# Steps of the Hyena filters put behind every one and a half experts of the first expert stage

## The chip, the cores and the metric

The kernel runs on one core of a Trainium2 chip. The metric is the device time of one execution in microseconds (us); lower is better. A core has five engines that run side by side, each through its own list of instructions in order: TensorE (PE in the profile; its weight loads are shown as PEld), VectorE (DVE), ScalarE (ACT), GpSimd (POOL) and SyncE (SP). Semaphores order them against each other. Sixteen DMA engines move data between the main memory and the on-chip buffers; SyncE and GpSimd issue the transfers that matter here, each from a queue of its own.

## What is computed

Two transformer blocks on 256 tokens of width 1024, in float32. Every attention or mixing layer is followed by a mixture of experts. Two parts matter here.

The first expert stage, of the first block: a router picks 2 of 32 experts for each token, and each expert is a gated network with 512 hidden units.

```python
def expert_block(args):
    xb, e = args
    return (jax.nn.silu(xb @ w1[e]) * (xb @ w3[e])) @ w2[e]
```

The filters of the second block's Hyena layer: a small network of the position (33 features, three layers of 64 with sines) gives 2 x 2 filters for each of the 1024 channels; they are damped by a decay, normalised by their sum of absolute values, and convolved with the tokens much later. They depend on no token, so their spectra can be computed at any time before that layer.

## The kernel before

**Order of the stages.** Block 1 (attention and recurrence), the first expert stage (`moe_phase` with `l` None), the second block's attention, its expert stage (16 smaller experts), the Hyena layer, a third expert stage. The filters are computed inside the first expert stage, and the Hyena layer reads their spectra from a scratch tensor in main memory (`spectra`).

**The first expert stage.** The stage has 32 experts of 64 slots each (a rare overflow has a path of its own). The weights come through a ring of six buffers of 2 MB (`ring`, issued on SyncE at L1827 and L1853): per expert two buffers of up weights (w1 and w3) and, from the third expert on, one of down weights, half of those of an expert pair. A buffer is loaded again when TensorE has done its last matmul with it. For expert `e`, `up_unit` multiplies the gathered tokens by the up weights, 16 matmuls of 512 columns in four units (L288); `evac` copies the result on ScalarE (L293); `turn` transposes it on TensorE (L300); `silu` (L306, ScalarE) and `act` (L311, VectorE) form the hidden values; `down_unit` (L378) multiplies those of an expert pair by the down weights; ScalarE scales the rows (L367), and GpSimd sends them to main memory with an indirect transfer (L369). `gather` (L259) picks and normalises tokens with one-hot matmuls for eight experts at a time: for the first eight before the stage's experts begin, and for each later group among the matmuls of the last expert of the group before.

`Moe.run` writes this sequence out by hand. It is traced inside `manual_schedule()`, so its own order stays as written. Everything that is traced outside is placed by a planner, which follows data, buffers and its own estimates of time, and puts an instruction with nothing to wait for where the engine would otherwise be idle in its plan.

**The filters.** `moe_phase` is given a function `after`, here `filters`, and calls it once the sequence up to the last expert is traced. Its instructions are to come after two others of the same engine (`issue_after`): on TensorE after `m.ready`, the last matmul of the first gather, and on VectorE after `last`. `issue_after(i)` binds only those instructions that run on the engine of `i`. `filter_first` loads a Fourier matrix and the small network's weights, and computes the network (L1619). Then come 16 units, one for each of two filter orders and eight blocks of 128 channels. A unit (`filter_spectrum`) is a generator with three parts:

1. load w4 (64 KB, two buffers, L1630) and the decay `dec` (128 KB, one buffer, L1632), both from GpSimd's queue; two matmuls (L1635); multiply by the decay on VectorE (L1637); sums of absolute values on ScalarE (L1641); normalise, and form sum and difference on VectorE (L1642 to L1649);
2. four transposes (L1654) and a copy on ScalarE to `ftk` (L1656);
3. eight matmuls with the Fourier matrix (L1662), a copy on ScalarE (L1665) into a buffer of the tag `hd`, which has two buffers shared with part 1, and a write of 256 KB from GpSimd's queue to `spectra` (L1666).

`filters` runs 18 steps. Step `n` traces part 3 of unit `n - 2`, part 2 of unit `n - 1` and part 1 of unit `n`. The tiles of the filters lie in the pool `pl`. After it is closed, the pool `m1o` takes its space; it holds the gate row `g2row` and the buffers `vw` into which the experts' rows are read back at the end of the stage (L1951). A float32 matmul shows as two records in the trace, a transpose as one.

Of the kernel before, what the change touches and what calls it, by code (L numbers as in the profile page):

```python
# [29 lines left out]
CAP = 64  # L30
# [5 lines left out]
class Ctx:  # L36


    def __init__(self, tc, es):
        self.tc, self.nc = tc, tc.nc  # L40
        self.n = 0
        self.last = [None] * 3
        self.const = es.enter_context(self.pool("const"))
        self.ps = {}
# [42 lines left out]
def make_consts(k):  # L87
    nc, c = k.nc, k.const
    jp = k.t(c, [P, P], I32, "jp")
    nc.gpsimd.iota(jp, pattern=[[1, P]], base=0, channel_multiplier=-1)  # L90
    k.ident = k.t(c, [P, P], F32, "ident")
    nc.vector.tensor_scalar(k.ident, jp, 0.0, None, op0=ALU.is_equal)
    k.before = k.t(c, [P, P], BF16, "before")
    nc.vector.tensor_scalar(k.before, jp, 0.0, None, op0=ALU.is_gt)
    k.ones_bf = k.t(c, [P, P], BF16, "ones_bf")
    nc.vector.memset(k.ones_bf, 1.0)
    k.io64 = k.t(c, [P, CAP], F32, "io64")
    nc.gpsimd.iota(k.io64, pattern=[[1, CAP]], base=1, channel_multiplier=0, allow_small_or_imprecise_dtypes=True)
    k.io96 = k.t(c, [P, 96], F32, "io96")
    nc.gpsimd.iota(k.io96, pattern=[[1, 96]], base=0, channel_multiplier=0, allow_small_or_imprecise_dtypes=True)  # L100

    k.place = k.t(c, [P, 2, 2], F32, "place")
    nc.gpsimd.iota(k.place, pattern=[[T, 2], [P, 2]], base=1, channel_multiplier=1, allow_small_or_imprecise_dtypes=True)
    k.down = k.t(c, [P, 8], F32, "down")
    nc.vector.tensor_scalar(k.down, k.io96[:, :8], -1.0, 8.0, op0=ALU.mult, op1=ALU.add)
# [126 lines left out]
class Moe:  # L232


    def __init__(self, k, es, name, r, h2h, h2l, load, NE, FF, Y):
        self.k, self.nc, self.r = k, k.nc, r

        self.Y, self.ND = Y, NE // 2 - (1 if FF == 512 else 2)
        self.h2h, self.h2l = h2h, h2l
        self.load = load  # L240
        self.NE, self.FF, self.name = NE, FF, name
        self.sb = es.enter_context(k.pool(name + "sb", 2))
        self.acc = None
        self.first = True
        self.xg, self.oh, self.st = {}, {}, {}

# [27 lines left out]
    def x_of(self, e, c):  # L274
        g, i = divmod(e, GE)
        return self.xg[g][c][:, i * CAP:(i + 1) * CAP]

    def up_unit(self, e, u, w, x_of=None):


        s = self.state(e)
        if u == 0:
            s["p"] = self.k.bank()
        for j in range(2):
            c = 2 * u + j
            x = x_of(c) if x_of else self.x_of(e, c)
            for a in range(2):
                self.nc.tensor.matmul(s["p"][a * CAP:(a + 1) * CAP, :self.FF], x, w(a, c), start=(c == 0), stop=(c == 7))  # L288

    def evac(self, e):  # L290
        s = self.state(e)
# [544 lines left out]
def residual(k, pool, x, out, grow, h):  # L836

    nc = k.nc
    for t in range(2):
        tmp = k.t(pool, [P, 512], F32, "otmp", bufs=2)  # L840
        nc.vector.tensor_tensor(tmp, out[t], grow[:, h * 512:(h + 1) * 512], op=ALU.mult)
        xs = x[:, t, h * 512:(h + 1) * 512]
        nc.vector.tensor_tensor(xs, xs, tmp, op=ALU.add)
# [14 lines left out]
def row_in(k, pool, d, i, name):  # L858

    o = k.t(pool, [P, D], F32, name)  # L860
    k.nc.gpsimd.dma_start(o, d[i:i + 1].broadcast_to([P, D]))
    return o
# [891 lines left out]
def ffn_in(k, tmp, rp, x, M):  # L1754

    nc = k.nc
    r = rms_rows(k, rp, x, "rx")
    wr, NL = M["wr"], M["wr"].shape[2]
    pl = [k.bank() for _ in range(2)]
    xT = k.t(tmp, [P, 8, T], F32, "h2T")  # L1760
    for c in range(8):
        if c % 2 == 0:
            pb = k.acc()
        pt = pb[:, c % 2 * T:c % 2 * T + T]
        for t in range(2):
            nc.tensor.transpose(pt[:, t * P:(t + 1) * P], x[:, t, c * P:(c + 1) * P], k.ident)
        if str(c) in EVD:
            nc.vector.tensor_scalar(xT[:, c], pt, M["s"][:, c:c + 1], None, op0=ALU.mult)
        else:
            nc.scalar.activation(xT[:, c], pt, AF.Copy, scale=M["s"][:, c:c + 1])  # L1770
    for c in range(8):
        for t in range(2):
            nc.tensor.matmul(pl[t][:, :NL], xT[:, c, t * P:(t + 1) * P], wr[:, c], start=(c == 0), stop=(c == 7))  # L1773
    return pl, r
# [96 lines left out]
def moe_phase(k, I, x, l, M, after=None, store=None):  # L1871

    nc, tc = k.nc, k.tc
    NE, FF = (32, 512) if l is None else (16, 256)
    pre = "m1" if l is None else f"n{l}"
    with ExitStack() as es:
        ph = Phase(k, es)
# [35 lines left out]
        with ExitStack() as e1:  # L1913
# [9 lines left out]
            pl, r = ffn_in(k, tmp, rp if l is None else tmp, x, M)  # L1923
# [6 lines left out]
        with ExitStack() as e1:  # L1930
            m = Moe(k, e1, pre, R, h2h, h2l, load, NE, FF, Y)
            m.fetch = fetch
            m.scale, m.shift = M["s"], M["sh"]
            m.start(oh)
            with tc.issue_after(m.gathers.ins):
                R.gates()
            run = m.run()
            with (tc.manual_schedule() if str(l) in MAN else ExitStack()):
                next(run)
            if after:  # L1940
                with tc.issue_after(m.ready.ins), tc.issue_after(last.ins), ExitStack() as e2:
                    after(ph("pl", 2, es=e2))
            with (tc.manual_schedule() if str(l) in MAN else ExitStack()):
                list(run)
            op = m.vpool = ph(pre + "o", es=e1)
            with tc.issue_after(last.ins):
                g2 = row_in(k, op, M["g2"], 0, "g2row")
            for h, t in ((0, 0), (0, 1), (1, 0), (1, 1)):
                y, c = k.t(op, [P, 2, 512], F32, "vw", bufs=2), slice(h * 512, (h + 1) * 512)
                with tc.issue_after(m.sent.ins):  # L1950
                    nc.gpsimd.dma_start(y, Y.rearrange("(c t p) d -> t p c d", c=2, p=P)[t][:, :, c])  # L1951
                with tc.issue_after(m.acted.ins):
                    nc.vector.tensor_tensor(y[:, 0], y[:, 0], y[:, 1], op=ALU.add)
                    nc.vector.tensor_tensor(y[:, 0], y[:, 0], g2[:, c], op=ALU.mult)
                    nc.vector.tensor_tensor(x[:, t, c], x[:, t, c], y[:, 0], op=ALU.add)

            def add():
                for h in range(2):
                    residual(k, op, x, [m.acc[t][h] for t in range(2)], g2, h)
                    if store:  # L1960
                        store(h)

            add()
            m.overflow(add)
            k.newt = None
# [342 lines left out]
def body(tc, I, out):  # L2308
    nc = tc.nc
    with ExitStack() as es:  # L2310
        k = Ctx(tc, es)
        make_consts(k)
        k.ones = k.t(k.const, [P, P], F32, "ones")
        nc.vector.memset(k.ones, 1.0)
        x = k.t(es.enter_context(k.pool("xp")), [P, 2, D], F32, "xres")
        k.ada = [k.t(k.const, [P, 48], F32, f"ada{l}") for l in range(2)]
        k.scratch = tc.dram_tile([2, T, 8, 2, P], F32, name="spectra")
        b2 = Block2(k, I, x)
        M = {}

        def rows(m, name, pool, ada, j, *args):

            if j == 9:
                m.update(moe_prep(k, pool, name, *args))
            elif j == 11:
                m["g2"] = rows_out(k, pool, ada[:, 40:48], f"g2{name}")

        def prep1(b, j):
            rows(M.setdefault(None, {}), 0, b.pf, b.mod, j, k.col("norm2_w"), b.mod, k.wr[0], k.row("b1"))

        def prep2(m, l, pool, j):
            rows(m, 1 + l, pool, k.ada[l], j, b2.gffn[l], k.ada[l], k.wr[1 + l], k.row("b2")[:, 20 * l:20 * l + 20])

        block1(k, I, x, b2, prep1)
        def filters(pl):
            b2.filter_first(pl)
            units = [b2.filter_spectrum(pl, *divmod(n, 8), k.scratch) for n in range(16)]
            for n in range(18):
                for u in units[max(n - 2, 0):n + 1]:
                    next(u)  # L2340

        moe_phase(k, I, x, None, M[None], filters)
        M[0] = mla(k, I, x, b2, prep2)
        moe_phase(k, I, x, 0, M[0])
        M[1] = hyena(k, I, x, b2, prep2)

        def store(h):
            cols = slice(h * 512, (h + 1) * 512)
            nc.sync.dma_start(out.rearrange("b (t p) d -> p (b t) d", p=P)[:, :, cols], x[:, :, cols])

        moe_phase(k, I, x, 1, M[1], store=store)


# [16 lines left out]
```

## Time and profile before

| what | value |
|---|---|
| time, median of 3 runs | 1477.58 us |
| lowest and highest of them | 1474.06 and 1480.67 us |
| profiled execution, time | 1470.14 us |
| profiled execution, span from first to last instruction | 1468.4 us |
| mean granted TensorE clock, as a share of 2.4 GHz | 0.949 |
| TensorE busy | 1307.5 us (89% of the span) |
| VectorE busy | 532.4 us (36%) |
| ScalarE busy | 471.8 us (32%) |
| moved by DMA | 459.01 MB, mean 313 GB/s |

The profile is one execution on the chip, recorded by the hardware. "L288" is line 288 of the kernel. Busy time counts an engine's instructions and not its waits; matmuls overlap and their ends are modelled, so a TensorE that is busy all the time need not be at its peak. The time of the execution is 1.7 us longer than the span of its instructions. The first expert stage lies between about 300 and 850 us of the span.

### The profile page before, as it was taken

What the parts mean: (1) busy time and instruction counts of PE and PEld (TensorE: products, weight loads), DVE (VectorE), ACT (ScalarE), POOL (GpSimd) and SP (SyncE); (2) the same over time, 40 slices, a digit from 0 to 9 for tenths busy, and PEclk for the clock granted to TensorE, in tenths of its full rate; (3) what the DMA queues carried; (4) which work ended last, traced back from release to release, by engine and by line L of the source; (5) the groups of instructions that cost most, each with busy time, mean ns of one, the idle gap of its engine ahead of it and who ended that gap; (6) DMA issues with size and microseconds to landing.
All of it is one profiled execution on the core that took longest, in us unless ns stands there. A gap on an engine that the chain in (4) does not pass through costs nothing. (4 is left out here: it accounts for less than half of the span.)

```text
span 1468.4 us, 18609 instructions
## 1 busy us (share of the span) xinstructions
PE 1307.5 (89%) x7225; PEld 754.8 (51%) x7225; DVE 532.4 (36%) x1525; ACT 471.8 (32%) x903; POOL 90.0 (6%) x135
## 2 busy tenths in 40 slices
PE   5899999989989999988988568998997599988995
PEld 2676576653445553323322244656553588756552
DVE  2554655451322220000000267445002677673004
ACT  2473433341233322211211145434231444324321
POOL 0000000010111210000000100000001000000000
PEclk9899989999989999999999879998999699997998
DMA  8566724379999999999999867568999565729995
GB/s 318 197 206 243 295 92 171 131 275 429 411 367 347 357 336 412 426 423 427 424 425 425 317 244 270 174 229 355 421 422 413 211 259 196 277 91 418 421 417 231
DMA packets 64944, 459.01 MB, mean 313 GB/s; under 512 B 9638, under 2 KB 9942, under 8 KB 32720
## 3 DMA queue, kind: packets, MB, share of 16 engines
q1 hardware_dynamic: 52496, 424.97, 73.3%
q0 software_dynamic: 11920, 32.04, 5.7%
q8 instruction: 60, 0.98, 0.3%
q10 hardware_dynamic: 432, 0.72, 0.2%
q14 instruction: 36, 0.29, 0.1%
HBM read 440.89 MB, written 25.71 MB: 318 GB/s over the span
## 5 line engine op out<-in xcount | busy, mean ns | idle before, releaser
L288 PE MATMUL bank<-ring,xg 128*64 128x512 f32 (+1 forms) x2048 | 355.0, 492 | 20.1 <-DMA ring<-in_w_dram 15.6
L288 PEld LDWEIGHTS bank<-ring,xg 128*64 128x64 f32 x2048 | 142.8, 137 | 207.1 <-issue 137.6
L378 PE MATMUL bank<-ring,a 128*64 128x512 f32 x768 | 204.6, 601 | 7.4 <-DMA ring<-in_w_dram 7.4
L311 DVE TENSOR_TENSOR a<-bank,sg 128x256 f32<-128x256 f32 (+1 forms) x64 | 22.9, 358 | 476.1 <-ACT sg L306 292.4
L819 DVE TENSOR_TENSOR wl<-ra,wh 128x1024 fp32r<-128x1024 f32 (+1 forms) x77 | 93.3, 1216 | 74.5 <-ACT wh L817 73.8
L817 ACT ACTIVATE wh<-ra 128x1024 fp32r<-128x1024 f32 (+1 forms) x77 | 80.5, 1052 | 118.2 <-PE acc L832 39.9
L293 ACT ACTIVATE s<-bank 128x512 f32<-128x512 f32 (+1 forms) x64 | 31.4, 491 | 247.3 <-PE bank L288 247.3
L378 PEld LDWEIGHTS bank<-ring,a 128*64 128x64 f32 x768 | 55.3, 136 | 102.4 <-issue 88.2
L899 PE MATMUL fill<-rb,cpad 128*32 128x512 f32 x384 | 66.9, 653 | 22.7 <-DMA rb<-in_ada_w_dram 17.1
L269 ACT ACTIVATE xg<-bank,mcols 128x512 f32<-128x512 f32 x64 | 49.8, 778 | 66.6 <-PE bank L259 63.7
L367 ACT ACTIVATE y<-bank,gts 128x512 f32<-128x512 f32 x54 | 37.1, 687 | 75.1 <-PE bank L378 75.1
L1688 PE MATMUL acc<-hTh,wh 128*128 128x256 f32 x192 | 55.5, 292 | 0.0
L1688 PE MATMUL acc<-hTh,wl 128*128 128x256 f32 x192 | 55.3, 293 | 0.2 <-DVE wl L819 0.2
L1688 PE MATMUL acc<-hTl,wh 128*128 128x256 f32 x192 | 54.0, 284 | 0.0
L306 ACT ACTIVATE sg<-bank 128x256 f32<-128x256 f32 (+1 forms) x64 | 21.0, 328 | 90.3 <-PE bank L300 90.3
L259 PE MATMUL bank<-oh,h2h 128*128 128x512 f32 x128 | 46.1, 443 | 3.3 <-DVE oh L226 3.3
L300 PEld LDWEIGHTS bank<-ident,s 128*128 128x128 f32 x192 | 19.8, 140 | 46.3 <-issue 34.6
L1662 PE MATMUL acc<-ftk,dftf 128*128 128x128 f32 x256 | 36.0, 287 | 7.8 <-ACT ftk L1656 7.8
L259 PE MATMUL bank<-oh,h2l 128*128 128x512 f32 x128 | 42.5, 415 | 0.0
L832 PE MATMUL acc<-wh,hTh 128*128 128x512 f32 (+1 forms) x96 | 39.1, 408 | 3.6 <-ACT hTv L801 3.6
L1662 PEld LDWEIGHTS acc<-ftk,dftf 128*128 128x128 f32 x256 | 30.8, 192 | 22.2 <-ACT ftk L1656 12.1
L832 PE MATMUL acc<-wh,hTl 128*128 128x512 f32 (+1 forms) x96 | 38.5, 401 | 0.0
(679 smaller groups left out, 2061.4 us busy)
## 6 DMA issues: line engine op xcount, KB each, us to landing
ring<-in_w_dram SPq DMA_DIRECT2D x64, 2048.0 KB, 16.2
ring<-in_moe_w_in_dram SPq DMA_DIRECT2D x32, 2048.0 KB, 19.0
ring<-in_w_dram SPq DMA_DIRECT2D x62, 1024.0 KB, 18.4
rb<-in_ada_w_dram SPq DMA_DIRECT2D x48, 1024.0 KB, 6.8
ring<-in_moe_w_down_dram SPq DMA_DIRECT2D x32, 1024.0 KB, 19.3
rb<-in_w_mod_dram SPq DMA_DIRECT2D x16, 1024.0 KB, 7.3
ra<-in_hy_w_in_dram SPq DMA_DIRECT2D x12, 1024.0 KB, 7.8
ra<-in_w_in_dram SPq DMA_DIRECT2D x20, 512.0 KB, 3.6
```

The source lines that it names most:

```text
L259: i = nc.tensor.matmul(self.gp, h[:, t, c * P:(c + 1) * P], oh[:, t], start=(a == t == 0), stop=(a == t == 1))
L269: self.gathers = nc.scalar.activation(xg, self.gp, AF.Identity, scale=self.scale[:, c:c + 1], bias=self.shift[:, c:c + 1])
L288: self.nc.tensor.matmul(s["p"][a * CAP:(a + 1) * CAP, :self.FF], x, w(a, c), start=(c == 0), stop=(c == 7))
L293: self.nc.scalar.activation(s["s"], s["p"][:, :self.FF], AF.Copy)
L367: nc.scalar.activation(s["y"][:, h * 512:(h + 1) * 512], s["d", h], AF.Copy, scale=s["gt"])
L378: self.nc.tensor.matmul(q["d", h][i * CAP:(i + 1) * CAP], self.state(2 * p + i)["av"][:, c], w[:, i], start=(c == 0), stop=(c == nk - 1))
L817: k.last[0] = k.nc.scalar.activation(wh[:, :, :n], w, AF.Copy)
L819: k.last[1] = k.nc.vector.tensor_tensor(wl[:, :, :n], w, wh[:, :, :n].bitcast(F32), op=ALU.subtract)
L832: k.last[2] = k.nc.tensor.matmul(out, x, y[:, j, c0:c0 + n], start=(kt == 0 and a == 0), stop=(kt == KT - 1 and a == 2))
L899: nc.tensor.matmul(pr[32 * g:32 * g + 32], k.cpad[:, l, 4 * q + g], wq[:, g], start=(q == 0), stop=(q == 1))
L1662: nc.tensor.matmul(pt[:, (2 * f + n) * P:(2 * f + n + 1) * P], self.fwd[:, t, n, f * P:(f + 1) * P], tk[:, n, t], start=(t == 0), stop=(t ...
L1688: nc.tensor.matmul(acc[i][:, :T], y[:, jj, i * P:(i + 1) * P], self.hT[x][:, kt], start=(kt == 0 and a == 0), stop=(kt == 7 and a == 2))
```

## The change

`Moe` keeps, for each expert, the last up matmul that it traced (`mark`). `moe_phase` hands these to `filters`, and step `n` is traced with the order that it comes after the mark of expert 1 + 3n // 2: experts 1, 2, 4, 5, 7, 8 and so on, the last step behind expert 26. The mark is an instruction of TensorE, so the order holds for what a step does on TensorE. `filter_first` is traced as before, and the two orders that hold for all of `filters` stay.

```diff
@@ class Moe, __init__
-        self.acc = None
+        self.acc, self.mark = None, {}
@@ class Moe, up_unit
             for a in range(2):
-                self.nc.tensor.matmul(s["p"][a * CAP:(a + 1) * CAP, :self.FF], x, w(a, c), start=(c == 0), stop=(c == 7))
+                self.mark[e] = self.nc.tensor.matmul(s["p"][a * CAP:(a + 1) * CAP, :self.FF], x, w(a, c), start=(c == 0), stop=(c == 7))
@@ moe_phase
                 with tc.issue_after(m.ready.ins), tc.issue_after(last.ins), ExitStack() as e2:
-                    after(ph("pl", 2, es=e2))
+                    after(ph("pl", 2, es=e2), m.mark)
@@ body
-        def filters(pl):
+        def filters(pl, mark):
+
             b2.filter_first(pl)
             units = [b2.filter_spectrum(pl, *divmod(n, 8), k.scratch) for n in range(16)]
             for n in range(18):
-                for u in units[max(n - 2, 0):n + 1]:
-                    next(u)
+                with tc.issue_after(mark[1 + 3 * n // 2].ins):
+                    for u in units[max(n - 2, 0):n + 1]:
+                        next(u)
```

## Rows read from the trace of the kernel before

**Rows 1.** The profile's page, first line.

```profile
span 1468.4 us, 18609 instructions
```

**Rows 2.** Busy time by stretch: start:end, length, busy us (instructions), granted clock, DMA share, rate.

```profile
340.00:380.00 40.00, 40.00 (x182) 13.37 (x179) 9.58 (x25) 8.09 (x16) 1.69 (x3) 1.00 1.01 425
380.00:420.00 40.00, 32.97 (x157) 15.94 (x155) 9.30 (x29) 9.20 (x27) 8.03 (x12) 0.87 1.01 403
420.00:560.00 140.00, 139.23 (x707) 69.86 (x704) 32.68 (x99) 42.93 (x103) 25.51 (x38) 1.00 0.93 348
560.00:640.00 80.00, 79.38 (x366) 29.76 (x366) 3.77 (x13) 17.24 (x28) 3.00 (x3) 1.00 1.01 425
640.00:820.00 180.00, 156.68 (x667) 53.74 (x668) 6.99 (x21) 25.92 (x45) 5.83 (x6) 1.00 1.01 424
```

The five busy times are those of PE, PEld, DVE, ACT and POOL.

**Rows 3.** Waits of TensorE's matmuls, 420 to 560 us: total, times, longest.

```profile
PE acc L1662 <- ACT ftk L1656: 0.8, 1, 0.8
```

**Rows 4.** Waits of TensorE's matmuls, 640 to 820 us.

```profile
PE bank L288 <- DMA ring<-in_w_dram: 15.6, 18, 1.2
...
```

**Rows 5.** Matmuls of two lines of the filters, duration and first and last start.

```profile
L1635 PE MATMUL acc<-fh,w x64: 376/376/480, 378.5 to 536.4; 64*128 64x256 f32 x64
...
L1662 PE MATMUL acc<-ftk,dftf x256: 275/275/579, 385.7 to 550.9; 128*128 128x128 f32 x128
```

**Rows 6.** ScalarE in order of time, evacuations of experts 14, 17 to 19, 26, 27, 28, 31.

```profile
569.30 0.60 ACT L293 ACTIVATE s<-bank 128x512 f32<-128x512 f32 x1 [6.21 <-PE bank L288]
...
612.34 0.60 ACT L293 ACTIVATE s<-bank 128x512 f32<-128x512 f32 x1 [7.37 <-PE bank L288]
623.38 0.60 ACT L293 ACTIVATE s<-bank 128x512 f32<-128x512 f32 x1 [6.21 <-PE bank L288]
634.42 0.60 ACT L293 ACTIVATE s<-bank 128x512 f32<-128x512 f32 x1 [6.24 <-PE bank L288]
...
739.57 0.60 ACT L293 ACTIVATE s<-bank 128x512 f32<-128x512 f32 x1 [8.43 <-PE bank L288]
754.37 0.60 ACT L293 ACTIVATE s<-bank 128x512 f32<-128x512 f32 x1 [8.39 <-PE bank L288]
769.12 0.60 ACT L293 ACTIVATE s<-bank 128x512 f32<-128x512 f32 x1 [8.42 <-PE bank L288]
...
815.12 0.60 ACT L293 ACTIVATE s<-bank 128x512 f32<-128x512 f32 x1 [8.44 <-PE bank L288]
```

**Rows 7.** TensorE in order of time, one unit's worth and what follows it.

```profile
463.38 1.16 PE L1662 MATMUL acc<-ftk,dftf 128*128 128x128 f32 x8
...
467.05 3.65 PE L288 MATMUL bank<-ring,xg 128*64 128x512 f32 x16
```

**Rows 8.** DMA issues, 380 to 420 us: count, KB each, median us to landing.

```profile
ring<-in_w_dram SPq DMA_DIRECT2D x3, 2048.0 KB, 17.0
...
spectra<-hd POOLq DMA_DIRECT2D x3, 256.0 KB, 11.0
dec<-in_k_decay_dram POOLq DMA_DIRECT2D x4, 128.0 KB, 9.1
w<-in_hy_f_w_dram POOLq DMA_DIRECT2D x4, 64.0 KB, 7.8
```

**Rows 9.** DMA issues, 420 to 560 us.

```profile
ring<-in_w_dram SPq DMA_DIRECT2D x14, 2048.0 KB, 9.5
...
spectra<-hd POOLq DMA_DIRECT2D x13, 256.0 KB, 7.1
```

**Rows 10.** GpSimd's queue in order of time, the gate row.

```profile
552.81 0.57 POOL L861 DMA_DIRECT2D g2row<-g  x1
```

**Rows 11.** All engines in order of time, 406.5 to 408.5 us, a stall.

```profile
406.89 0.59 ACT L1665 COPY hd<-acc 128x512 f32<-128x512 f32 x1 [9.66 <-DMA spectra<-hd]
407.38 0.59 ACT L1656 COPY ftk<-acc 128x512 f32<-128x512 f32 x1
...
408.02 0.80 PE L1662 MATMUL acc<-ftk,dftf 128*128 128x128 f32 x2 [7.03 <-ACT ftk L1656]
```

**Rows 12.** Waits of all engines, 420 to 560 us.

```profile
DVE hd L1637 <- DMA dec<-in_k_decay_dram: 18.0, 4, 5.6
```

## Prediction

> **What bounds the kernel now.** The profiled execution takes 1470.14 us, of which 1468.4 us are span [rows 1]. I read the table of stretches first, over the first expert stage, because all edits lie there. The reader is to look at two columns, the DMA rate and TensorE's busy time [rows 2]. Three regimes show. From 340 to 420 us and from 560 to 820 us the core's DMA engines are full (share 1.01) and move 424 to 425 GB/s, with a dip to 403 between 380 and 420. From 420 to 560 they are not full: share 0.93, 348 GB/s, and there TensorE is busy for 139.23 of 140 us. From 640 on TensorE is busy for 156.68 of 180 us only, at a granted clock of 1.00, so it runs at 2.4 GHz and still has 23.3 us to spare.
>
> Then the waits of TensorE. Between 420 and 560 it waits for no weights; the one wait listed is 0.8 us for a filter's copy [rows 3]. Between 640 and 820 its longest wait in total is for the ring of expert weights [rows 4]. So the bound changes inside one stage: TensorE in the stretch with the filters, the weight stream elsewhere. The filters sit just there: first matmul of a unit at 378.5 us, last one at 550.9 us [rows 5].
>
> The pace of the experts gives the prices. ScalarE evacuates each expert once (L293). From 623.38 to 634.42 us is one expert with TensorE running through: 11.04 us. From 754.37 to 769.12 is one at the pace of the weights: 14.75 us. From 569.30 to 612.34 are three experts with a whole group's gather among them: 43.04 − 3 × 11.04 = 9.92 us for the gather, once in eight experts [rows 6].
>
> **The change, part by part.** Nothing is removed and no instruction is added: keeping the last up matmul of each expert in `mark` is bookkeeping at build time, and the argument `mark` costs nothing on the chip. What moves are 16 filter units in 18 steps. An order after expert 1 + 3n//2 is put on what step n issues on TensorE, the engine of the mark; its VectorE, ScalarE and GpSimd work, loads and writes included, follows by data and buffers alone.
>
> On TensorE, one unit's worth (16 of the 256 records of L1662, 4 of L1654, 4 of the 64 of L1635 [rows 5]) takes from 463.38 to 467.05 us, so 3.67 us, and 16 units 58.7 us [rows 7]. Per step in the steady state, with 1.5 experts: 1.5 × 11.04 + 3.67 + 9.92 × 1.5/8 = 22.1 us of TensorE. The weights of 1.5 experts take 1.5 × 14.75 = 22.1 us of DMA. A unit's own transfers are 256 + 128 + 64 KB [rows 8], 0.459 MB, which at 424.5 GB/s is 1.08 us, plus what they slow the stream by, below 0.6 us: 23.8 us. TensorE keeps 1.7 us of slack a step. So after the change the weight stream is the bound nearly throughout, and what TensorE does for the filters hides behind it. If that cover were gone, the 58.7 us would show.
>
> What can be won is what the DMA engines now lose: 40 × (1 − 403/424.5) = 2.0 us between 380 and 420, and 140 × (1 − 348/424.5) = 25.2 us between 420 and 560, together 27.2 us. The bytes stay the same, so the transfers' own time is in that already.
>
> What is won depends on why they lose it. Of the 25.2 us, (1.01 − 0.93)/1.01 × 140 = 11.1 us is idle engine time, because slots of the ring come free late; this goes away with TensorE's lag. The other 14.1 us are busy but slow. Two bounds. If all of it is the price of the filters' small transfers, it moves with them: between 420 and 560 there are 13 writes of spectra with their loads [rows 9], about 12 units by bytes, so 1.2 us a unit, 19.2 us for 16, and the gain is 27.2 − 19.2 = 8.0 us. If none of it is, the gain is 27.2 us. The nearest row to the state after the change is 380 to 420: filters beside a ring that is full of requests (a ring load lands 17.0 us after its issue there, 9.5 us between 420 and 560). There 3 writes, 4 decay loads and 4 weight loads were issued [rows 8], 1.57 MB or 3.4 units, and the loss is 2.0 us: 0.6 us a unit. I take that: 16 × 0.6 = 9.6 us, gain 27.2 − 9.6 = **17.6 us**.
>
> On this point the Trainium skill, "DMA: Bandwidth & Descriptors", Specifications, gives 512 bytes as the smallest transfer that still runs at line rate. The filters' pieces are runs of 512 bytes to 1 KB by the shapes in the code, so by that rule a unit costs its bytes alone and the gain would be 27.2 us. The 403 GB/s of the row say that this is too kind.
>
> Edits I cost at nothing, with their cover. The three tensors a unit loads are issued from GpSimd's queue, which also sends each expert pair's result rows (L369) and the gate row g2row. With a step every 22 us these stand between issues that are one step apart; dec has a single buffer, and its next load can go out once the VectorE product (L1637) is done, with 14.75 us at least before the next step and 9.1 us to landing [rows 8]. Queued behind that product on VectorE is the experts' L311, for which the down matmuls wait. g2row now goes out at 552.81 us, behind the filters [rows 10]; its buffer reuses their space, so it will go out behind the last step, after expert 26. That one is evacuated at 739.57 us now, and the last expert at 815.12 [rows 6], so g2row will still be there some 70 us before the stage's closing sums need it. The first steps cannot follow experts 1, 2 and 4: the features they need end at 378 us, beside expert 5, and I expect steps 0 to 3 close together there, as now. That costs nothing while the ring is full. The stall in that place, 7.03 us of TensorE behind a ScalarE copy that waits 9.66 us for an earlier spectrum's write [rows 11], stood in a stretch where the DMA share was 1.01, so losing it adds nothing to the 17.6 us.
>
> Against the profiled execution: 1470.14 − 17.6 = 1452.5 us. The median of the three runs shown, 1477.58 us, lies 7.4 us above that execution; the forecast for a median is 1477.6 − 17.6 = **1460 us**.
>
> **The rivals.**
>
> *The transfers carry their full price along* (no measurable change, 0.5% being 7.4 us, about what a measurement of this kernel can tell from nothing). 1.2 us a unit or somewhat more, gain 0 to 8 us, 1470 to 1478. For it: from 460 to 560 the DMA engines are nearly full and still slow. Against it: the same transfers cost half of that beside a full ring, and the wait that disappears is idle time as well. 0.18.
>
> *The transfers cost only their bytes*: gain 27 us, 1450. This is also what the 512 bytes of the Trainium skill's page would give. Against it stands the dip to 403. 0.10, counted with the faster ones.
>
> *Each step makes TensorE wait* (slower). Its queue is in order; a step's matmul that waits for ScalarE, VectorE or a load holds the experts behind it. Place: L1662 behind the copy L1656, and L311 behind L1637 waiting for dec. It has 1.7 us of slack a step. Beyond that every us costs 16 us: from 2.8 us a step the gain is gone, from 3.3 us the kernel is slower by over 0.5%. With the longest wait of VectorE for dec in the profile, 5.6 us [rows 12], at every step: 16 × (5.6 − 1.7) − 17.6 = +45 us, 1522. For it: such waits exist now. Against it: they come from units packed two to an expert, and the change puts at least one expert between two steps. 0.10.
>
> *The change does not spread them as it says.* The mark is only a lower bound, and a step goes where the written order of TensorE has room; steps that slide behind the last expert would show at 3.67 us each, so five of them would eat the gain: 1478, more of them slower. Against it: the steps now fill the places where TensorE later waits for the ring, and these places recur at every expert up to the last. 0.04.
>
> **How the numbers follow.** Forecast, with a loss of 0.3 to 1.2 us a unit, gain 8 to 22 us: 0.58. The rival in which steps slide is split by how many do: 0.02 still gain, 0.01 come out even, 0.01 slower. Faster by over 0.5%: 0.58 + 0.10 + 0.02 = 0.70. Within 0.5%: 0.18 + 0.01 = 0.19. Slower: 0.10 + 0.01 = 0.11. The predicted time is the forecast's, 1460 us. The range reaches from the full 27.2 us (1450) to almost no gain (1476); what it leaves out is slower cases and the last bit of the first rival.
>
> **What would show it.** Right: between 340 us and the end of the stage no long stretch under 410 GB/s; units' matmuls from about 380 to 720 us; experts evenly at 14.8 to 16.5 us; expert 31 evacuated near 797 us, not 815.12; every later stage earlier by the same amount. The price of the transfers shows as the DMA rate with filters against 424 after them. Wrong: waits at L1662, L1637 or L311 of several us per step, a clock below 1.00 in the stage, units after the last expert, or 400 GB/s and less with a full share for as long as the filters run.

## The result, and the profile after

The kernel with the change takes 1454.7 us (median of 4 runs, 1450.3 to 1460.1), the one before 1478.88 us (median of 4, 1474.06 to 1480.67). The ratio is 0.9851, with a 95% interval of 0.9820 to 0.9882: 22 us less, with 17 to 27 us in the interval. The forecast was 17.6 us less, 1460 us.

The two profiled executions differ by less, 1470.14 and 1460.1 us. That lies within the scatter from run to run: the one before was shorter than all of its four timed runs, the one after the longest of its four. The stage itself is a better measure, so I use one number from here on: the **stage time**, from the evacuation of the first expert to that of expert 31 on ScalarE (L293). Before it is 815.12 [rows 6] − 329.96 = 485.2 us. After, in ScalarE's order of time:

```profile
332.65 0.60 ACT L293 ACTIVATE s<-bank 128x512 f32<-128x512 f32 x1 [6.06 <-PE bank L288]
...
409.31 0.58 ACT L1665 COPY hd<-acc 128x512 f32<-128x512 f32 x1 [9.59 <-DMA spectra<-hd]
...
509.08 0.60 ACT L293 ACTIVATE s<-bank 128x512 f32<-128x512 f32 x1 [5.39 <-PE bank L288]
520.18 0.60 ACT L293 ACTIVATE s<-bank 128x512 f32<-128x512 f32 x1 [6.24 <-PE bank L288]
535.99 0.60 ACT L293 ACTIVATE s<-bank 128x512 f32<-128x512 f32 x1 [5.45 <-PE bank L288]
...
799.11 0.60 ACT L293 ACTIVATE s<-bank 128x512 f32<-128x512 f32 x1 [8.43 <-PE bank L288]
```

799.11 − 332.65 = 466.5 us, 18.7 us less. The stage began 2.7 us later in this execution, so its end stands 16.0 us earlier; the rest of the way to the span's end, through stages whose code is the same, gives 6 us back (653.3 us before, 659.2 after). In the twelve other executions below this rest takes 654.6 to 662.4 us, so the 6 us are scatter:

```profile
span 1458.3 us, 18601 instructions
```

The table of stretches, in the columns of [rows 2] and with the same first five stretches, then three that cut the last one finer:

```profile
340.00:380.00 40.00, 40.00 (x184) 13.33 (x182) 8.69 (x23) 8.26 (x16) 1.64 (x2) 1.00 1.01 424
380.00:420.00 40.00, 35.18 (x163) 15.56 (x160) 10.62 (x32) 9.88 (x28) 7.23 (x11) 0.91 1.01 405
420.00:560.00 140.00, 140.00 (x660) 60.74 (x656) 19.29 (x58) 36.50 (x75) 15.67 (x22) 1.00 1.01 414
560.00:640.00 80.00, 80.00 (x388) 33.71 (x388) 11.55 (x36) 18.08 (x40) 9.60 (x13) 1.00 1.01 415
640.00:820.00 180.00, 163.38 (x735) 62.31 (x733) 17.49 (x48) 32.72 (x63) 13.56 (x17) 1.00 0.97 404
...
640.00:700.00 60.00, 59.69 (x275) 25.02 (x274) 6.55 (x18) 16.20 (x33) 5.26 (x7) 1.00 1.01 421
700.00:740.00 40.00, 40.00 (x196) 16.37 (x196) 3.60 (x15) 6.53 (x15) 3.05 (x4) 1.00 1.01 425
740.00:800.00 60.00, 50.02 (x212) 16.18 (x211) 2.02 (x6) 7.54 (x14) 2.04 (x2) 1.00 1.01 424
```

The DMA share is 1.01 from 340 to 800 us: the hole of 0.93 and 348 GB/s between 420 and 560 us is gone. What is left is a shallow dip to 414, 415 and 421 GB/s while filters run, and 424 to 425 once they are done. The 404 in the fifth row is no dip: its last 20 us lie behind the end of the stage. What the dip costs, from these rows: 40 × (1 − 405/424.5) + 140 × (1 − 414/424.5) + 80 × (1 − 415/424.5) + 60 × (1 − 421/424.5) = 1.8 + 3.5 + 1.8 + 0.5 = 7.6 us. Of the 27.2 us that the DMA engines lost before, that leaves 19.6 us, and the stage shows 18.7.

The waits of TensorE's matmuls from 420 to 700 us, the whole list (before, [rows 3] and [rows 4]):

```profile
PE bank L288 <- DMA ring<-in_w_dram: 0.3, 1, 0.3
```

TensorE is busy without a gap, the DMA engines are full, and neither waits for the other. The two bounds have met. The units are spread as written, from 381.2 to 728.4 us, where [rows 5] ended at 550.9:

```profile
L1635 PE MATMUL acc<-fh,w x64: 375/376/481, 381.2 to 698.4; 64*128 64x256 f32 x64
...
L1662 PE MATMUL acc<-ftk,dftf x256: 274/275/378, 388.4 to 728.4; 128*128 128x128 f32 x128
```

Where the time came from is seen in the intervals between the evacuations of neighbouring experts (us, read from ScalarE's order of time):

| from expert | before | after |
|---|---|---|
| 0 to 5 | 8.4, 7.7, 11.0, 11.8, 14.5 | 8.4, 7.7, 11.0, 11.8, 14.5 |
| 5 to 13 | 31.2, 23.5, 17.9, 22.5, 20.8, 21.6, 21.3, 16.1 (174.9) | 27.2, 17.0, 18.7, 17.6, 11.1, 15.8, 15.8, 11.1 (134.2) |
| 13 to 31 | 11.0 to 18.4 (256.9) | 11.1 to 20.2 (278.9) |

Experts 5 to 13 give 40.7 us, experts 13 to 31 take 22.0 us back.

### The profile page after: what moved, and what is told of

Read it like the earlier page. It is cut to its first block, busy times and chain, and to the rows that moved or that the text cites. A ratio compares the mean times of both kernels' runs of the same rounds, so it can differ in the third digit from the quotient of the medians.

```text
span 1458.3 us, 18601 instructions
## 1 busy us (share of the span) xinstructions
PE 1310.4 (90%) x7225; PEld 757.7 (52%) x7225; DVE 532.4 (37%) x1525; ACT 471.0 (32%) x903; POOL 90.5 (6%) x135
## 5 line engine op out<-in xcount | busy, mean ns | idle before, releaser
L378 PE MATMUL bank<-ring,a 128*64 128x512 f32 x768 | 207.0, 607 | 2.9 <-DMA ring<-in_w_dram 2.9
L293 ACT ACTIVATE s<-bank 128x512 f32<-128x512 f32 (+1 forms) x64 | 31.3, 490 | 240.3 <-PE bank L288 240.3
L378 PEld LDWEIGHTS bank<-ring,a 128*64 128x64 f32 x768 | 55.5, 137 | 94.7 <-issue 85.6
L300 PE MATMUL bank<-ident,s 128*128 128x128 f32 x192 | 35.4, 294 | 6.7 <-ACT s L293 6.7
L832 PE MATMUL acc<-wl,hTh 128*128 128x512 f32 (+1 forms) x96 | 38.5, 401 | 0.0
## 6 DMA issues: line engine op xcount, KB each, us to landing
ring<-in_w_dram SPq DMA_DIRECT2D x64, 2048.0 KB, 20.2
```

Source lines behind the costliest of these rows:

```text
L293: self.nc.scalar.activation(s["s"], s["p"][:, :self.FF], AF.Copy)
L300: self.nc.tensor.transpose(pm[:, c * P:(c + 1) * P], s["s"][:, c * P:(c + 1) * P], k.ident)
L378: self.nc.tensor.matmul(q["d", h][i * CAP:(i + 1) * CAP], self.state(2 * p + i)["av"][:, c], w[:, i], start=(c == 0), stop=(c == nk - 1))
L832: k.last[2] = k.nc.tensor.matmul(out, x, y[:, j, c0:c0 + n], start=(kt == 0 and a == 0), stop=(kt == KT - 1 and a == 2))
```

## The experiments

Twelve kernels, each against the kernel before on the same chip. A stage time is from one profiled execution. Experts 20 to 31 took 165.7 to 166.6 us in the five kernels with no filter work left there (before, 5, 7, 8 and 10), so differences of about 1 us between stage times are read as none.

| kernel | median, us | ratio to before, 95% | stage, us |
|---|---|---|---|
| before | 1476.3 to 1478.9 | 1 | 485.2 |
| after | 1454.7 | 0.9851 [0.9820, 0.9882] | 466.5 |
| 1 one step per expert | 1467.03 | 0.9945 [0.9921, 0.9968] | 477.1 |
| 2 after, four experts later | 1457.57 | 0.9867 [0.9833, 0.9902] | 464.8 |
| 3 after, less TensorE work | 1456.75 | 0.9868 [0.9838, 0.9899] | 465.5 |
| 4 after, half the decay loads | 1456.32 | 0.9864 [0.9837, 0.9891] | 463.1 |
| 5 after, no filters | 1433.81 | 0.9702 [0.9665, 0.9739] | 440.7 |
| 6 after, no transfers of the units | 1439.62 | 0.9736 [0.9697, 0.9776] | 448.2 |
| 7 before, no transfers of the units | 1464.56 | 0.9907 [0.9876, 0.9939] | 474.8 |
| 8 before, less TensorE work | 1480.66 | 1.0018 [0.9996, 1.0040] | 490.1 |
| 9 one step per expert, from expert 5 | 1454.41 | 0.9837 [0.9814, 0.9859] | 465.4 |
| 10 before, three writes fewer | 1472.12 | 0.9960 [0.9942, 0.9978] | 479.3 |
| 11 experiments 2 and 4 together | 1453.71 | 0.9836 [0.9812, 0.9859] | 461.8 |
| 12 after, every spectrum written twice | 1469.74 | 0.9955 [0.9933, 0.9976] | 476.1 |

### 1. One step behind every expert

```diff
-                with tc.issue_after(mark[1 + 3 * n // 2].ins):
+                with tc.issue_after(mark[1 + n].ins):
```

> The steps come one behind every expert instead of one behind every one and a half, so the units are over by expert 16. Stage time below means from the first to the last expert's evacuation: 485.2 us before, 466.5 us after the change. Theory (TensorE's lag was the loss, and a unit costs the weight stream about 1.6 us wherever it stands): an expert then takes TensorE 11.04 + 3.67 + 1.24 = 16.0 us and the stream 14.75 + 1.6 = 16.4 us, so the stream is still the bound: stage 464 to 470 us, ratio to the kernel before 0.982 to 0.990. Rival (the density of small transfers slows the stream): the density lies half way between before and after, so about half of the gain is gone: stage 474 to 478 us, ratio 0.991 to 0.996.

More than half of the gain is gone, 10.6 of 18.7 us of the stage, about as the rival said. But the density is not shown to be the reason, because the kernel is not what I had in mind: the features are ready only beside expert 5, when the marks of experts 1 to 4 are past. Eight units land on experts 5 to 8, with intervals of 30.9, 23.5 and 17.9 us, those of before; behind them each expert has one unit and takes 15.8 us. The stretches behind the pile:

```profile
420.00:460.00 40.00, 40.00 (x194) 19.93 (x193) 6.17 (x17) 14.86 (x31) 5.99 (x9) 1.00 0.87 339
460.00:560.00 100.00, 100.00 (x489) 43.62 (x487) 20.47 (x63) 22.91 (x58) 15.37 (x23) 1.00 1.01 405
```

### 9. One step behind every expert, from the fifth

```diff
-                with tc.issue_after(mark[1 + 3 * n // 2].ins):
+                with tc.issue_after(mark[5 + n].ins):
```

> One step behind every expert again, but from expert 5 on, so that the first eight units no longer stand at experts 5 to 8. The run with one step per expert from expert 1 on had a stage of 477.1 us, and its experts 5 to 8 were as long as those of the kernel before. Theory (the loss there was TensorE's lag at the bunched units, 10 us; elsewhere one unit per expert costs TensorE 11.04 + 4.75 + 1.24 = 17.0 us against 16.4 us of the stream, and the ring covers that small lag): stage 465 to 471 us. Rival (one unit per expert is too dense for the DMA engines): 474 to 479 us, as with the first of these.

The same density without the pile, and the stage is as short as after's:

```profile
420.00:560.00 140.00, 140.00 (x670) 61.94 (x670) 23.92 (x72) 37.49 (x84) 19.47 (x28) 1.00 1.01 413
```

With experiment 1 this shows what the change cures: a pile of units on few experts puts TensorE behind the stream of weights, buffers of the ring come free late, and the DMA engines go short (0.87 there, 1.01 here). One and a half experts per step or one makes no difference here. Experiment 1 also has the stall of [rows 11] ahead of its pile, 6.7 us of TensorE, and this one has not; by experiment 10 that is worth some 4 of the 11.7 us between the two.

### 2. The same spread, four experts later

```diff
-                with tc.issue_after(mark[1 + 3 * n // 2].ins):
+                with tc.issue_after(mark[5 + 3 * n // 2].ins):
```

> All steps are moved four experts later, with the same spacing: they no longer bunch at experts 5 and 6, and the stall of several us behind a spectrum's write with the lower clock after it should vanish. Theory (the stall stands where the stream is the bound anyway, so it costs nothing): stage 464 to 469 us as after the change, ratio 0.982 to 0.989. Rival (the stall and the clock are part of the remaining loss): stage 457 to 461 us, ratio 0.976 to 0.981.

After still has the stall of [rows 11], 9.59 us of ScalarE at 409.31 in the rows above, and TensorE's granted clock is 0.91 in that stretch, with 35.18 of 40 us busy: behind the stall it is at the 1.2 GHz level for a while (eight records of L378 take 3.68 us, 1.89 us just ahead of it). Four experts later it does not occur: the interval 5 to 6 is 13.1 us and not 27.2. The stage gains 1.7 us, little more than a stage time can tell, so after the change the stall is hidden.

### 10. Before, with the first three writes left out

```diff
-        nc.gpsimd.dma_start(scratch[o][:, c].rearrange("(f p) n d -> p f (n d)", f=2), sp.rearrange("p f n d -> p f (n d)"))
+        if 8 * o + c > 2:
+            nc.gpsimd.dma_start(scratch[o][:, c].rearrange("(f p) n d -> p f (n d)", f=2), sp.rearrange("p f n d -> p f (n d)"))
```

> The kernel before without the writes of the first three spectra (left out; the Hyena layer reads other data of the same size). The ScalarE copy for which TensorE stood 7.03 us at expert 6 then has no write to wait for, and the clock should not fall there; 0.79 MB fewer are written. Theory (a stall ahead of the stretch in which TensorE is the bound makes TensorE late for all of that stretch): stage 7 to 10 us shorter, 475 to 478 us, all of it in the interval between the evacuations of experts 5 and 6. Rival, which the forecast held (the stall stands where the stream is full and is hidden): only the bytes, 2 us: stage 483 us.

Before the change the same stall was not free. Without the writes that cause it the interval 5 to 6 falls from 31.2 to 25.6 us and the next one by 0.7 us, the others up to expert 18 stay, and the stage is 5.9 us shorter. That lies between the two forecasts. The bytes left out, 0.79 MB, are 1.9 us of it at 424.5 GB/s. The rest is DMA time that is no longer lost where TensorE is the bound: 360 GB/s between 420 and 560 us in place of the 348 of [rows 2], which is 140 × 12/424.5 = 4.0 us.

```profile
420.00:560.00 140.00, 139.23 (x709) 69.53 (x709) 32.11 (x99) 42.55 (x102) 25.49 (x39) 1.00 0.95 360
```

The granted clock from 380 to 420 us is 1.00 here, 0.87 in [rows 2]. TensorE's longest wait from 380 to 470 us is now another one, so the gain is less than the 7.03 us of the stall:

```profile
PE acc L1654 <- DVE fs L1648: 2.9, 1, 2.9
```

### 7. Before, without the units' transfers

```diff
-        nc.gpsimd.dma_start(w4, self.I["hy_f_w4_2"][0]. ...)
-        nc.gpsimd.dma_start(dec, self.I["k_decay"][c * P:(c + 1) * P])
+        if o == c == 0:  (both loaded once, and kept for all units)
...
-        nc.gpsimd.dma_start(scratch[o][:, c]. ...)
...
-                        nc.sync.dma_start(K[o, h], k.scratch[o] ...)
+                        nc.sync.dma_start(K[o, h] ..., I["k_decay"] ...)
```

> The kernel before without the units' transfers, in the same way. On TensorE the units stand at experts 5 to 12 as in the kernel before. Theory (there TensorE's lag was the bound): TensorE is late all the same and the weights wait for their buffers; only what the units waited for their loads goes: stage 470 to 480 us, ratio 0.990 to 0.997. Rival (the small transfers, packed together, made the DMA engines slow, and moving them apart is what the change won): the loss goes with the transfers: stage under 460 us, ratio under 0.983.

All intervals are those of before but 5 to 6, 21.7 us in place of 31.2. So TensorE alone sets the pace of experts 6 to 13, whatever the transfers do. And the DMA engines are short *and* slow without them:

```profile
380.00:420.00 40.00, 40.00 (x206) 20.77 (x202) 11.73 (x36) 12.30 (x32) 1.01 (x1) 1.00 1.00 423
420.00:460.00 40.00, 40.00 (x194) 19.20 (x191) 7.80 (x23) 14.04 (x30) 0.99 (x1) 1.00 0.87 339
460.00:560.00 100.00, 99.22 (x513) 48.37 (x512) 22.56 (x69) 26.63 (x67) 3.50 (x4) 1.00 0.82 314
```

Divided by its share, a full set of engines would move 390 and 383 GB/s behind 420 us here, 374 in [rows 2] between 420 and 560 us, and 420 where the ring is full of requests. Some three quarters of the slowness per busy engine are there without the units' transfers beside the ring. From 380 to 420 us, where the ring is full of requests, it is the other way: 423 GB/s here against 403 before (405 in experiment 10, with most of the transfers and without the stall), so that dip, from which the forecast took its 0.6 us a unit, is the transfers'.

### 6. After, without the units' transfers

The edit is that of experiment 7, in the kernel after.

> The changed kernel without the units' transfers: the weights and the decay of one unit are loaded once and used by all, no spectrum is written, and the Hyena layer reads other data of the same size. All of TensorE's, VectorE's and ScalarE's work stays. Theory (the stream is the bound and a unit costs it 1.6 us): the stage falls nearly to the floor without filters, 437 to 445 us, though TensorE (22.1 us a step) and the weights (22.1 us) are then equal: ratio 0.967 to 0.973. Rival (TensorE is the bound after the change): stage stays within 5 us of 466 us, ratio 0.982 or more.

18.3 us less, between the two forecasts, and not the 25.8 us that leaving out the filters altogether gives (experiment 5; 24.6 of them are the filters' own), because TensorE takes over. From expert 7 to expert 27 every interval is that of after to within 0.5 us: in both kernels TensorE sets the pace there. The gain sits at the two ends, 7.4 us at experts 5 to 7, where the stall is gone with the writes, and 10.2 us behind expert 27, where TensorE after the change waits for the ring again (9.3 us from 730 to 800 us). No matmul waits from 420 to 700 us, and the DMA engines have some room:

```profile
460.00:560.00 100.00, 100.00 (x472) 41.91 (x470) 13.43 (x37) 25.16 (x52) 3.88 (x4) 1.00 0.99 412
640.00:770.00 130.00, 129.31 (x606) 51.41 (x604) 9.48 (x31) 27.30 (x53) 5.44 (x6) 1.00 1.00 413
```

### 3. After, with less work on TensorE

```diff
-        pt = k.fbank()
-        (the four transposes of L1654 and the copy to ftk)
...
-        (the eight matmuls of L1662 and the copy of L1665)
+        sp = hd.rearrange("p d (n c) -> p d n c", n=2)
```

> The changed kernel without the second and third part of each unit on TensorE and ScalarE (the transposes, the Fourier matmuls and their copies are left out; what is written as the spectrum is the filter itself, so the Hyena layer gets other numbers). All transfers stay. TensorE has 42 us less to do in the stage. Theory (TensorE's filter work is hidden behind the stream): stage 463 to 468 us, as after the change, ratio 0.981 to 0.988. Rival (TensorE still sets part of the time): stage down by 10 us or more, under 457 us, ratio under 0.978.

No gain beyond what a stage time can tell (1.0 us). The time freed on TensorE turns into waits for the ring, 420 to 700 us:

```profile
PE bank L288 <- DMA ring<-in_w_dram: 20.4, 16, 4.1
```

The DMA rate stays near after's 414 GB/s, so the dip there does not come from a TensorE that is late:

```profile
420.00:560.00 140.00, 129.39 (x540) 47.67 (x538) 19.43 (x59) 29.58 (x63) 16.75 (x23) 0.98 1.01 416
```

So in the kernel after the stream sets how long the stage takes, and TensorE's filter work is hidden, but, by experiment 6, only just.

### 5. After, without the filters

```diff
-        moe_phase(k, I, x, None, M[None], filters)
+        moe_phase(k, I, x, None, M[None])
...
-                        nc.sync.dma_start(K[o, h], k.scratch[o] ...)
+                        nc.sync.dma_start(K[o, h] ..., I["k_decay"] ...)
```

> The changed kernel without any filter work in the stage; the Hyena layer reads other data of the same size instead of the spectra. This is the floor of the stage. Theory (after the change the filters cost only their transfers, 16 x 1.6 us and 1 to 2 us for the first loads): stage 466.5 - 27 = 437 to 442 us, ratio about 0.967. Rival (TensorE's 58.7 us are partly paid too): stage under 430 us, ratio under 0.960.

```profile
420.00:560.00 140.00, 126.48 (x551) 44.78 (x548) 7.03 (x24) 21.91 (x36) 4.85 (x5) 1.00 1.01 426
```

The stream alone runs at 426 GB/s. After's filters cost 466.5 − 440.7 = 25.8 us; before the change they cost 44.5 us. Some of that is not theirs: without them the gate row's transfer of 512 KB, 1.2 us at 424.5 GB/s, goes out at 302.20 us, ahead of the stage. That leaves 24.6 us, 1.54 us a unit.

### 4. After, with each decay block loaded once

```diff
-        dec = k.t(pool, [P, T], F32, "dec", bufs=1)
-        nc.gpsimd.dma_start(dec, self.I["k_decay"][c * P:(c + 1) * P])
+        if o == 0:
+            self.dec = k.t(pool, [P, T], F32, "dec", bufs=1)
+            nc.gpsimd.dma_start(self.dec, self.I["k_decay"][c * P:(c + 1) * P])
+        dec = self.dec
...
-            units = [b2.filter_spectrum(pl, *divmod(n, 8), k.scratch) for n in range(16)]
+            units = [b2.filter_spectrum(pl, n % 2, n // 2, k.scratch) for n in range(16)]
```

> The changed kernel with the units in the order block by block, both filter orders of a block one after the other, so that the decay of a block is loaded once and used twice: 8 loads of 128 KB fewer, the same arithmetic. Theory (the stream is the bound, each byte of the filters is paid): 8 x 0.131 MB at 424.5 GB/s is 2.5 us, with their share of the slowing 3 to 4 us: stage 462 to 464 us, ratio 0.3% below that of the change, 0.980 to 0.986. Rival (the small loads are hidden, only the writes slow the stream): stage 466 us, no difference from the change.

Eight loads fewer, 1.05 MB or 2.5 us at 424.5 GB/s, and the stage is 3.4 us shorter (experiment 11 against 2: 3.0). The times of the whole kernel can't tell so little.

### 12. After, with every spectrum written twice

```diff
         nc.gpsimd.dma_start(scratch[o][:, c].rearrange("(f p) n d -> p f (n d)", f=2), sp.rearrange("p f n d -> p f (n d)"))
+        nc.gpsimd.dma_start(k.scratch2[o][:, c].rearrange("(f p) n d -> p f (n d)", f=2), sp.rearrange("p f n d -> p f (n d)"))
...
+        k.scratch2 = tc.dram_tile([2, T, 8, 2, P], F32, name="spectra2")
```

> The changed kernel with each spectrum written twice, the second time to a tensor that nobody reads: 16 x 0.262 MB more from GpSimd's queue, 4.19 MB, nothing else. Theory (the stream is the bound and pays every byte): 4.19 MB at 424.5 GB/s is 9.9 us and 1 to 4 us of slowing: stage 477 to 481 us, ratio 0.991 to 0.997. Rival (there is still room on the DMA engines, as TensorE runs through): stage up by less than 5 us, under 471 us.

4.19 MB more make the stage 9.6 us longer; at 424.5 GB/s the bytes alone take 9.9 us. The 1 to 4 us of slowing on top did not come, and the rate does not fall below after's:

```profile
420.00:560.00 140.00, 140.00 (x660) 60.47 (x657) 19.20 (x58) 36.34 (x75) 19.89 (x28) 1.00 1.01 414
```

A write costs its bytes, then, and they are not hidden.

### 8. Before, with less work on TensorE

The edit is that of experiment 3, in the kernel before.

> The kernel before without the second and third part of each unit on TensorE and ScalarE (left out as in the run of the changed kernel without them); all transfers stay, and stand closer together than before (12 of 16 units at experts 5 and 6). Theory (TensorE's lag was the loss): TensorE's filter work is 17 us instead of 59 us, the ring covers that, and the stage comes down to about that of the change although nothing is spread: 464 to 472 us, ratio 0.981 to 0.991. Rival (dense small transfers are the loss): no gain or a larger loss, stage 480 us or more, ratio 0.996 or more.

The stage is 490.1 us, longer than before, as the rival said, but this did not isolate what it was meant to. With shorter units the planner put twelve of them on experts 5 and 6, and TensorE, in order, waited for their loads, 370 to 480 us:

```profile
PE acc L1635 <- DMA w<-in_hy_f_w_dram: 26.1, 8, 6.7
...
DVE hd L1637 <- DMA dec<-in_k_decay_dram: 38.5, 12, 5.6
```

From 380 to 480 us TensorE is busy for 73.88 of 100 us, at a granted clock of 0.81.

It does show the prediction's third rival at work: with units back to back the single `dec` buffer serves one every few us, and what saved the lag was lost to waiting.

### 11. Experiments 2 and 4 together

Both edits are shown above.

> Both small gains together: all steps four experts later, and the units block by block with one load of the decay for two. Theory (the stream is the bound, each byte is paid; the early stall is gone): stage 460 to 463 us, 0.3 to 0.4% below the changed kernel, ratio to the kernel before 0.980 to 0.986. Rival (TensorE, which waits for almost nothing between 420 and 700 us, is by now the bound): stage 464 to 466 us.

461.8 us is the shortest stage with all of the filters in it, 4.7 us below after's, and about the sum of the two single effects (1.7 + 3.4). By the ratios it can't be told from after: the intervals overlap.

## Why the prediction was right, and where its steps were off

**The bound and its cure: right, and shown.** TensorE, lagging behind a pile of units, starved the ring. Without the pile the DMA share is 1.01 and the stage 18.7 us shorter, against 17.6. Experiments 1 and 9 differ in the pile and in the stall ahead of it, and 11.7 us lie between them. Experiment 7 takes the small transfers away and leaves the pile: the intervals from expert 6 to 13 do not change.

**The idle 11.1 us: right. The 14.1 us "busy but slow": half right.** The upper bound of 1.2 us a unit took all of these as the price of the small transfers. Experiment 7 refutes it: most of the slowness is there without the units' transfers. Rate and landing time go together: a ring load landed 9.5 us after its issue in [rows 9], and 17.7 us after, from 420 to 700 us:

```profile
ring<-in_w_dram SPq DMA_DIRECT2D x36, 2048.0 KB, 17.7
```

That the engines are slow because few large loads are outstanding fits both, but was only argued; no run changed the depth of the ring alone.

**The price of a unit's transfers: right in size.** I took 1.08 us for the bytes and 0.6 us for slowing the stream. The dip after costs 7.6 us, 0.48 us a unit, and the two sum to 1.56 us; experiment 5 gives 1.54. The first rival asked for 1.2 us beyond the bytes, the second for none. By the 512-byte rule of the Trainium skill, "DMA: Bandwidth & Descriptors", Specifications, the gain would have been 27.2 us; 414 GB/s beside 424 does not agree, although the writes of experiment 12 do. That leaves the loads as the source of the 0.48 us; experiment 4 points there (3.4 us for 2.5 us of bytes), which is too little to call it shown.

**TensorE's price of a unit: too small.** I read 3.67 us from [rows 7], a unit in one piece. The same trace has another at 456.66 us, which parts the eight records of a group of down matmuls:

```profile
455.71 1.02 PE L378 MATMUL bank<-ring,a 128*64 128x512 f32 x2
...
459.06 1.93 PE L378 MATMUL bank<-ring,a 128*64 128x512 f32 x6
```

After the change this is the usual place. After, in TensorE's order of time, an expert without a unit and the start and the end of one with it:

```profile
508.86 1.89 PE L378 MATMUL bank<-ring,a 128*64 128x512 f32 x8
510.68 0.66 PE L300 MATMUL bank<-ident,s 128*128 128x128 f32 x4
511.27 1.94 PE L378 MATMUL bank<-ring,a 128*64 128x512 f32 x8
513.03 7.04 PE L288 MATMUL bank<-ring,xg 128*64 128x512 f32 x32
519.90 1.02 PE L378 MATMUL bank<-ring,a 128*64 128x512 f32 x2
520.85 2.05 PE L1662 MATMUL acc<-ftk,dftf 128*128 128x128 f32 x16
522.74 0.27 PE L1654 MATMUL acc<-ident,fs 128*128 128x128 f32 x1
522.94 1.93 PE L378 MATMUL bank<-ring,a 128*64 128x512 f32 x6
524.80 0.66 PE L300 MATMUL bank<-ident,s 128*128 128x128 f32 x4
525.39 1.94 PE L378 MATMUL bank<-ring,a 128*64 128x512 f32 x8
527.26 0.33 PE L1654 MATMUL acc<-ident,fs 128*128 128x128 f32 x1
527.42 0.38 PE L1654 MATMUL acc<-ident,fd 128*128 128x128 f32 x2
527.74 1.13 PE L1635 MATMUL acc<-fh,w 64*128 64x256 f32 x4
528.79 7.09 PE L288 MATMUL bank<-ring,xg 128*64 128x512 f32 x32
```

The expert without a unit took 520.18 − 509.08 = 11.10 us, the one with it 535.99 − 520.18 = 15.81, so a unit costs 4.7 us. Its own instructions are 522.94 − 520.85 = 2.09 and 528.79 − 527.26 = 1.53 us, and the rest is in the down matmuls: eight records in one go take 510.68 − 508.86 = 1.82 us; parted after the second one they take 0.95 + 1.86 = 2.81, so 0.99 us more. Where they are parted counts. The eight records are four matmuls of 64 columns, from two calls of `down_unit`; the two of one call, one for each expert of the pair, follow each other (L378). Parted behind the fourth record, by a gather, they take only 1.01 + 1.01 = 2.02 us:

```profile
557.12 1.08 PE L378 MATMUL bank<-ring,a 128*64 128x512 f32 x4
558.13 0.74 PE L259 MATMUL bank<-oh,h2h 128*128 128x512 f32 x2
...
560.17 1.08 PE L378 MATMUL bank<-ring,a 128*64 128x512 f32 x4
561.18 0.66 PE L300 MATMUL bank<-ident,s 128*128 128x128 f32 x4
```

One such matmul alone takes 0.95 us and two in a row 1.01, so what the unit loses is the overlap of two matmuls. A step is thus 1.5 × 11.04 + 4.7 + 1.9 = 23.2 us of TensorE against 23.8 of the stream: the slack is 0.6 us and not 1.7. It held, as the wait of 0.3 us shows, but it is why taking the transfers away in experiment 6 gives only 18.3 us: 16 × 0.6 = 9.6 us, near the 10.2 us behind expert 27, and the 7.4 us at the stall.

**The stall that "adds nothing".** After, it is hidden (experiment 2). Before, it was not (experiment 10: some 4 us beyond the bytes left out), and the reason I gave, a full DMA share in its stretch, is no reason. TensorE was the bound from there on, and what it lost at 407 us came back as DMA time lost behind 420 (348 GB/s there, 360 without the stall). The forecast did not suffer, because the sum counts that loss there, once.

**Smaller points.** Steps 0 to 3 do stand together beside experts 5 and 6. `g2row` goes out behind the last step and before the rows that are read back at the end of the stage, without harm:

```profile
730.39 0.59 POOL L861 DMA_DIRECT2D g2row<-g  x1
...
811.68 1.53 POOL L1951 DMA_DIRECT2D vw<-m1Y  x2 [5.68 <-DMA m1Y<-y,idx]
```

Experts do not pass evenly at 14.8 to 16.5 us but at 11.1, 15.8, 15.8 in turn, since a unit goes to TensorE in one lump and the ring evens it out. The granted clock is 1.00 in all stretches from 420 us on, so the 2.4 GHz level held. One stretch stays under the 410 GB/s that I set as a sign: 380 to 420 us, at 405. "Every later stage earlier by the same amount" can't be judged from one execution of each kernel: the rest behind the stage scatters by 9 us (653.3 to 662.4).

## What to carry to other kernels

Two engines that are both near their limit must be balanced in every stretch, not on average: give the filler work out so that the engine's sum per step stays below the stream's, and look at where the first steps *can* start, since marks that are past bind nothing and the steps pile up. A full DMA share beside a stall does not make the stall free; ask which engine is the bound behind it, and try it by taking its cause away. Where the two bounds have met, as here, cutting TensorE's filter work alone gave nothing that a stage time can tell, and cutting all of the units' transfers alone gave 18 of some 25 us that the filters still cost: to go further, both have to fall.

## What the runs showed of the hardware

DMA engines can be slow while they are busy, without the units' small transfers: 383 to 390 GB/s for a full share in experiment 7, 420 beside a full ring. And a filler put between two matmuls of 64 columns each that would have followed each other directly costs 0.99 us beyond its own time: 0.95 + 1.86 us for the eight records of L378 parted inside such a two, 1.82 us in one go. Parted between one two and the next, they took 2.02 us.
